# A decoder layer on one core: projection weights split six steps behind their loads, and two early output products placed behind the last value products

## The chip, the cores and the metric

The kernel runs on one core of one Trainium2 chip. The time is device microseconds of that core for one launch; of several launches the median is given. The trace is one execution taken by the hardware profiler.

## The reference, cut to what matters

One decoder layer over 2048 positions of width 1024: stick-breaking attention with 12 heads of 64, a four-head attention into 256 memory tokens, one output projection, layer norm, a squared-ReLU MLP of width 4096, and layer norm again.

```python
proj = x @ w_in_sb                      # q, k, v of 12 heads, and q_mem
z = q_block @ k.T * 64 ** -0.5          # 128 queries at a time, all earlier keys
log_stay = where(strict, log_sigmoid(-z), 0)
w = where(strict, exp(log_sigmoid(z) + sum of log_stay over the later keys), 0)
mix = w @ v
y = concat([mix, mem_out]) @ w_out
x = layer_norm(2 ** 0.25 * x + y)
x = layer_norm(2 ** 0.25 * x + square(relu(x @ w_up)) @ w_down)
```

## The kernel before, in words

Every product is done in float16 with both operands split into a high and a low half, so a weight tile that comes from memory in float32 is cut in two before TensorE (PE) may use it. `load_w` does that: it issues the load on SP's queue into a staging tile of tag "st" (three buffers), and hands two closures to `later`: `high` on ScalarE (ACT, L143), `low` one step after it on VectorE (DVE, L148). `load_cols` is its form for a 128-column piece of the input projection; `out_load`, which brings the rows of `w_out`, calls `load_w` with a 3 of its own.

Two heads are worked together as a pair p, from 0 to 5. `attention` writes the whole program of that part out by hand, step after step. One step is 128 queries of one pair against up to 512 keys: score products into two PSUM banks of tag "z" (four banks, L280), a sigmoid on ACT (L458), a scan on DVE (L466, the tile is "e"), a split of the weights on ACT and POOL (L317, L318), and a transpose by DMA from SP's queue (L319). A pair has 40 steps. Where keys and queries are of the same block, the first steps are short (128, 256, 384 keys), and some of their weights are transposed on PE (L327) and split on ACT and DVE (L161, L162, the tile is "w"). The value products (`gather`, L340, into a bank "av") of a block of keys come `BEHIND` = 4 steps after its last weights. Between the steps PE gets the projections of the next pair in portions, and the loads of the pair after that are put among them. `later(n, fn)` runs `fn` n steps on; what is due at a step is issued ahead of that step's scores. The order that results is nailed down: each instruction of an engine is tied to the one before it, on PE, DVE, ACT, POOL and SP alike.

The loads that stand inside the steps are those of the pairs 2 to 5, for v, k and q: twelve (names sv, wv and so on in the trace; sv2 is the staging tile of pair 2's value weights, wv2 its split halves).

Steps are counted through all segments, N of them. At step N, behind the last scores, `tail` issues the first 21 of 24 products of four output tiles (op12_0, op12_1, op13_0, op13_1; L670), which need all heads but the last pair, into the four "z" banks. The value products of the last block (av5_3) follow at step N + 4. Then DVE adds the end values (L301, the tile "om"), ACT and DVE split it (the tile m5_3), and the last three products of each output tile use it.

From there on the program is not written by hand: the building tool orders it by a simulated time of its own. It holds the rest of the output tiles (op14, op15, which need a "z" bank each that DVE has emptied, L677), the layer norms (L599 to L634), the left operands of the MLP (`left_operands`: sums "os" on DVE and POOL, transposes "ot" on PE at L732, evictions "op" on ACT at L161 and on DVE at L162), and the splits of the first MLP weights (L713, L714; "rt" from wu, "wr" from wd). The MLP's first product (upa, L830) uses PSUM banks that are given out anew, so it stands behind the last of these evictions.

Of the kernel before, what the change touches and what calls it, by code (L numbers as in the profile page):

```python
# [34 lines left out]
def trunk_layer(ctx: ExitStack, tc: tile.TileContext, x, mem, w_in, w_kv, w_out,  # L35
# [70 lines left out]
    def later(n, fn):  # L106
        if clock[0] is None:
            fn()
        else:
            due.setdefault(clock[0] + n, []).append(fn)  # L110

    def run(work):
        for _ in work:
            pass
# [17 lines left out]
    def load_w(key, src, shape, n, tag="ws"):  # L132

        s = sbt("st", shape, F32, f"s{key}")
        w = sbt(tag, [P, 2, D], F16, f"w{key}")
        W[key] = w
        with early():
            nc.sync.dma_start(s, src)
        flat = s if len(shape) == 2 else s.rearrange("p k f -> p (k f)")

        def high():
            with early():
                A.activation(w[:, 0, :], flat, AF.Copy, scale=SW)  # L143
                later(1, low)

        def low():
            with early():
                V.scalar_tensor_tensor(w[:, 1, :], flat, SW, w[:, 0, :], ALU.mult, ALU.subtract)  # L148

        later(n, high)  # L150

    def load_cols(w, c0, key, n=3):

        load_w(key, w[:, c0:c0 + P].rearrange("(k p) f -> p k f", p=P), [P, KT, P], n)

# [188 lines left out]
    def mem_attend():  # L344
        for hp in range(MP):
            load_cols(w_in, 3 * SBW + hp * P, f"qm{hp}")
            for c in range(NC):
                run(q_chunk(f"qm{hp}", c, f"qm{hp}_{c}"))
# [96 lines left out]
    def score(pair):  # L445

        t = pair[0]
        for u in pair:
            u.z = pst("z", "z" + u.name)
        score_pair([u.z[:, :t.W] for u in pair], qq[f"q{t.p}_{t.c}"], t.i,  # L450
                   lambda j: kk[t.p][j][:, t.pc * C:t.pc * C + t.W], not t.diag)
        if t.diag:
            for u in pair:
                T.matmul(u.z[:, t.W - P:t.W], lhsT=idb, rhs=mask, start=False, stop=True)

    def stay(pair):
        for t in pair:
            A.activation(t.z[:, :t.W], t.z[:, :t.W], AF.Sigmoid, scale=-SCORE)  # L458
# [3 lines left out]
    def scan(pair):  # L462
        for t in pair:
            t.e = sbt("et", [P, C], F32, "e" + t.name)
            init = SP if t.diag else carries[t.p, t.c, t.pc + 1][:, t.i, t.h:t.h + 1]
            V.tensor_tensor_scan(t.e[:, t.W - 1::-1], t.z[:, t.W - 1::-1], zero[:, 0:1].broadcast_to([P, t.W]), init,  # L466
                                 ALU.mult, ALU.add)
# [3 lines left out]
    def spread(pair):  # L471
        t = pair[0]
        key = t.p, t.c, t.pc
        if t.i == 0:
            carries[key] = sb.tile([P, TB, 2], F32, name="carry", bufs=3)
            for h in range(2):
                weights[key, h] = sbt("pw", [P, TB, 2 * TB, P], F16, f"w{t.p}_{t.c}_{t.pc}_{h}")
        if t.diag and t.i not in DMA_DIAG:
            turn_short([weights[key, h][:, t.i] for h in range(2)], [u.e[:, :t.W] for u in pair], "t" + t.name)
        for u in pair:  # L480
            if not t.diag or t.i in DMA_DIAG:
                turn(weights[key, u.h][:, t.i], u.e[:, :t.W], "t" + u.name)
            if t.pc > 0:
                A.activation(carries[key][:, t.i, u.h:u.h + 1], u.e[:, 0:1], AF.Copy)
# [3 lines left out]
    def gather(p, c, pc, sblk):  # L488

        if pc == c and sblk == 0:  # L490
            sums[p, c] = pst("av", f"av{p}_{c}")
        vt = vv[p, pc // 2]
        av_step(sums[p, c], lambda h, j: vt[:, pc % 2, j, sblk, h * HD:(h + 1) * HD],
                lambda h, j: weights[(p, c, pc), h][:, :, 2 * sblk + j, :],
                sblk if pc == c else 0, pc == c and sblk == 0, pc == 0 and sblk == TB - 1)
        if pc == 0 and sblk == TB - 1:
            later(1, lambda: store_mix(sums[p, c], c, p, f"m{p}_{c}", vend[p][:, c * TB:(c + 1) * TB]))
# [6 lines left out]
    BEHIND = 4  # L504

    def attention(segments, tail):

        first = nc.cur_bb.bb.instructions[-1] if nc.cur_bb.bb.instructions else None  # L510
        steps, starts = [], {}
        for blocks, done, units in segments:
            mine = [[Score(p, c, pc, h, i) for h in range(2)] for p, c in blocks for pc in range(c, -1, -1)
                    for i in range(TB)]
            starts[len(steps)] = units, len(mine), done
            steps += mine
        N = len(steps)
        share = [SHARE[0][t.i] if t.diag else SHARE[1] for t, _ in steps]
        own = [OWN[0][t.i] if t.diag else OWN[1] for t, _ in steps]
        for n, (t, _) in enumerate(steps):  # L520
            if t.i == TB - 1 and n + 1 + BEHIND < N:
                own[n + 1 + BEHIND] += VALUES[0] if t.diag else VALUES[1]

        def deal(begin, count, total):


            mine = range(begin, begin + count)
            low, high = 0, 10 * (total + sum(own))
            for _ in range(60):
                rate = (low + high) / 2  # L530
                parts = [max(0, rate * share[n] - own[n]) for n in mine]
                low, high = (rate, high) if sum(parts) < total else (low, rate)
            return [sum(parts[:k + 1]) for k in range(count)]

        work, spent, total = None, 0, 0
        for n in range(-1, N + BEHIND + 3):
            clock[0] = n
            if n in starts:
                if work is not None:
                    run(work)  # L540
                units, count, done = starts[n]
                begin, spent, total = n, 0, sum(k for k, _ in units)
                plan = deal(n, count, total / done)
                work = (cost for _, u in units for cost in u())
            for fn in due.pop(n, []):
                fn()
            if n + 1 < N:
                score(steps[n + 1])
                stay(steps[n + 1])
            if 0 <= n < N:  # L550
                scan(steps[n])
            if 0 <= n - 1 < N:
                spread(steps[n - 1])
                t = steps[n - 1][0]
                if t.i == TB - 1:
                    for sblk in range(TB):
                        later(BEHIND, lambda t=t, sblk=sblk: gather(t.p, t.c, t.pc, sblk))
            if work is not None:
                while spent < min(total, plan[min(n - begin, len(plan) - 1)]):
                    cost = next(work, None)  # L560
                    if cost is None:
                        spent = total
                        break
                    spent += cost
                if n >= N:
                    run(work)
            if n == N:
                tail()
        n += 1
        while due:  # L570
            clock[0] = n
            for fn in due.pop(n, []):
                fn()
            n += 1
        clock[0] = None
        ins = nc.cur_bb.bb.instructions
        last = {}
        on = first is None
        for i in ins:
            if on and i.engine in ENGINES:  # L580
                if i.engine in last:
                    tc.add_manual_dep(i, last[i.engine].name, ISSUE, reason="in order")
                last[i.engine] = i
            on = on or i is first
# [423 lines left out]
    def qkv_load(p, what):  # L1008
        return once(load_cols, w_in, {"q": 0, "k": SBW, "v": 2 * SBW}[what] + p * P, f"{what}{p}")
# [11 lines left out]
    for c in range(NC):  # L1021
        if c < len(kv_work):
            fn, hp, c0, nm = kv_work[c]
            load_cols(w_kv, c0, nm)
            fn(hp, nm)
        load_x(c)
# [73 lines left out]

    lastly = [out_proj((NC - 1) * TB + i, n) for i in range(TB) for n in range(NH)]

    def tail():
        free_banks[0] = ("z",)
        for work in lastly[:4]:
            for _ in range(3 * (NKO - 1)):
                next(work)

    attention(segments, tail)
    ops = {}  # L1110
    hot[0] = 1
# [12 lines left out]
    for half in range(NC // 2):  # L1124
        if half == 0:
            load_gb(g2, b2, [(gbs[:, 0], gbs[:, 1]), (gbs[:, 2], gbs[:, 3])])
        for f0 in range(0, NFP, GROUP):
# [16 lines left out]
            work = down(half, len(fps), hl, wr, f0 == 0, last)  # L1144
# [44 lines left out]
```

## Time and profile before

| | |
|---|---|
| median of 3 runs | 2434.29 us (2431.82 to 2435.8) |
| the profiled execution's own time | 2430.05 us |
| its span | 2428.3 us |
| PE busy | 2237.2 us (92%) |
| DVE busy | 1709.7 us (70%) |
| ACT busy | 1185.7 us (49%) |
| POOL busy | 1021.7 us (42%) |
| TensorE's mean granted clock | 0.975 of full speed |

The busy shares are means over stages with different limits. The steps of attention run from about 204 to 1073 us, the output projection's end and the start of the MLP from there to about 1200 us, the MLP to the end. A matmul's end is modelled, so a busy PE is not a PE at its peak; its waits are read from the times between its instructions.

### The profile page before, as it was taken

How to read it: one execution, taken by the hardware profiler on the slowest of the kernel's cores; microseconds unless marked ns; L12 is line 12 of the kernel's file. 1: busy time of each engine (PE TensorE's matmuls, PEld its weight loads, DVE VectorE, ACT ScalarE, POOL GpSimd, SP SyncE). 2: the span in 40 equal slices, each digit the busy share in tenths (PEclk: the TensorE clock that was granted, in tenths of full speed). 3: DMA queues.
4: the chain of work that ended last, by engine and by line, in shares of the span. 5: the costliest groups of instructions: out<-in, count | busy, mean ns of one | idle time of the engine just before them, and what ended most of it. 6: DMA issues, size and time to landing. Idle time of an engine off the chain costs nothing.

```text
span 2428.3 us, 34523 instructions
## 1 busy us (share of the span) xinstructions
PE 2237.2 (92%) x12032; PEld 1000.8 (41%) x12032; DVE 1709.7 (70%) x2385; ACT 1185.7 (49%) x2577; POOL 1021.7 (42%) x826
## 2 busy tenths in 40 slices
PE   7798999999989999997799999999997999999996
PEld 4343434344334343333344444444443444444443
DVE  4456777777776777779987888888676454555447
ACT  4456677776766656544544454445433322233321
POOL 0001656566564556564654456443443122211124
PEclk9899999999999999998999999999998999999998
DMA  7244888879887787876643445334565333323211
GB/s 260 44 85 90 154 162 152 162 137 163 150 160 143 165 173 170 167 178 183 220 165 114 142 152 182 133 115 149 169 194 190 105 109 96 108 87 96 96 44 70
DMA packets 606285, 342.03 MB, mean 141 GB/s; under 512 B 487840, under 2 KB 544672, under 8 KB 606112
## 3 DMA queue, kind: packets, MB, share of 16 engines
q1 hardware_dynamic: 606112, 339.84, 55.8%
q8 instruction: 94, 1.54, 0.3%
q14 instruction: 79, 0.65, 0.1%
HBM read 143.65 MB, written 77.59 MB: 91 GB/s over the span
## 4 chain that ended last, share of the span: by engine, by line
PE 58%; DVE 18%; issue 8%; ACT 7%; DMA 5%; POOL 3%; SPq 0%; ACTq 0%; DVEq 0%; POOLq 0%
PE dnb L906 7%; PE upb L830 7%; PE dnc L906 5%; PE dna L906 5%; PE upc L830 5%; PE upa L830 4%; PE pq L252 4%; PE z L280 4%; PE op L670 4%; PE av L340 3%; PE kp L252 3%; PE vp L252 3%; DVE wr L714 2%; DVE e L466 2%; POOL t L318 2%
## 5 line engine op out<-in xcount | busy, mean ns | idle before, releaser
L318 POOL TENSOR_TENSOR t<-e,t 128x512 f16<-128x512 f32 (+1 forms) x384 | 431.6, 1150 | 360.0 <-ACT t L317 293.0
L830 PEld LDWEIGHTS <-rt 128*128 128x128 f16 x2688 | 266.2, 99 | 387.7 <-issue 81.1
L906 PEld LDWEIGHTS <-hl 128*128 128x128 f16 x2736 | 267.4, 98 | 335.5 <-DVE hl L841 11.2
L466 DVE TENSOR_TENSOR_SCAN e<-z,carry,zero 128x512 f32<-128x512 f32 x288 | 350.4, 1265 | 44.5 <-ACT z L458 30.2
L921 POOL TENSOR_TENSOR acc<-acc,v 128x512 f32<-128x512 f32 x112 | 149.9, 1341 | 503.1 <-DVE acc L919 432.4
L458 ACT ACTIVATE z<-z 128x512 f32<-128x512 f32 (+1 forms) x480 | 226.6, 513 | 229.5 <-PE z L280 123.7
L830 PE MATMUL upb<-op,rt 128*128 128x512 f16 x1152 | 269.6, 383 | 13.0 <-DVE u L874 6.9
L906 PE MATMUL dnb<-wr,hl 128*128 128x512 f16 x1008 | 236.1, 380 | 0.0
L317 ACT ACTIVATE t<-e 128x512 f16<-128x512 f32 (+1 forms) x384 | 225.9, 616 | 7.7 <-DMA w<-t 6.9
L280 PE MATMUL z<-k,q 64*128 64x512 f16 (+3 forms) x1440 | 186.0, 349 | 32.3 <-DVE e L466 31.7
L830 PE MATMUL upa<-op,rt 128*128 128x512 f16 x768 | 184.8, 389 | 26.3 <-ACT u L863 19.3
L830 PE MATMUL upc<-op,rt 128*128 128x512 f16 x768 | 183.7, 387 | 16.1 <-DVE u L869 16.1
L670 PE MATMUL op<-wo,mx 128*128 128x512 f16 x720 | 171.6, 387 | 1.8 <-DVE acc L677 1.8
L466 DVE TENSOR_TENSOR_SCAN e<-z,zero 128x128 f32<-128x128 f32 (+1 forms) x192 | 147.0, 806 | 32.1 <-ACT z L458 24.9
L906 PE MATMUL dna<-wr,hl 128*128 128x512 f16 x672 | 155.0, 380 | 9.7 <-DVE hl L841 9.7
L906 PE MATMUL dnc<-wr,hl 128*128 128x512 f16 x672 | 161.1, 379 | 1.8 <-ACT hl L713 1.1
L340 PE MATMUL av<-w,v 128*64 128x512 f16 (+3 forms) x1440 | 145.9, 349 | 4.5 <-DMA w<-t 4.5
L252 PE MATMUL vp<-xT,wv 128*128 128x512 f16 x576 | 140.4, 388 | 0.0
L252 PE MATMUL pq<-xT,wq 128*128 128x512 f16 x576 | 138.7, 385 | 0.0
L252 PE MATMUL kp<-xT,wk 128*128 128x512 f16 x576 | 136.0, 380 | 0.0
L836 ACT ACTIVATE u<-u 128x512 f32<-128x512 f32 x96 | 60.3, 628 | 132.9 <-DVE u L874 78.6
L280 PEld LDWEIGHTS <-q 64*128 64x128 f16 x1440 | 55.4, 94 | 148.7 <-issue 104.7
(177 smaller groups left out, 3248.0 us busy)
## 6 DMA issues: line engine op xcount, KB each, us to landing
keptdown<-wr SPq DMA_DIRECT2D x106, 256.0 KB, 2.5
wr<-keptdown SPq DMA_DIRECT2D x106, 256.0 KB, 2.9
keptup<-rt SPq DMA_DIRECT2D x48, 512.0 KB, 3.0
rt<-keptup SPq DMA_DIRECT2D x48, 512.0 KB, 3.6
wu<-in_w_up_dram SPq DMA_DIRECT2D x32, 512.0 KB, 4.6
wd<-in_w_down_dram SPq DMA_DIRECT2D x32, 512.0 KB, 4.0
x<-in_x_dram SPq DMA_DIRECT2D x16, 512.0 KB, 10.3
acc<-in_x_dram SPq DMA_DIRECT2D x16, 512.0 KB, 5.2
```

What stands on the lines that cost most here:

```text
L252: T.matmul(pp, lhsT=wt[:, a, k, :], rhs=xs(xT, c, b, k), start=n == 0, stop=n == 3 * KT - 1)
L280: T.matmul(banks[h], lhsT=q[rows, a, i * P:(i + 1) * P], rhs=keys(b)[rows], start=n == 0, stop=stop and n == 2)
L317: A.activation(hi, src, AF.Copy)
L318: G.tensor_tensor(lo, src, hi, ALU.subtract)
L340: T.matmul(av[h * HD:(h + 1) * HD, i0 * P:].rearrange("p (t n) -> p t n", n=P), lhsT=vv(h, a), rhs=pT(h, b)[:, i0:, :], start=first and n ...
L458: A.activation(t.z[:, :t.W], t.z[:, :t.W], AF.Sigmoid, scale=-SCORE)
L466: V.tensor_tensor_scan(t.e[:, t.W - 1::-1], t.z[:, t.W - 1::-1], zero[:, 0:1].broadcast_to([P, t.W]), init, ALU.mult, ALU.add)
L670: T.matmul(pp, lhsT=lhs, rhs=W[f"o{k}"][:, kb, n * C:(n + 1) * C], start=m == 0, stop=m == 3 * NKO - 1)
L830: T.matmul(bv, lhsT=r[:, a, k, :], rhs=operand(ops, s, b, k), start=start and n == 0, stop=n == 3 * HB - 1, skip_group_check=not start)
L836: A.activation(t, t if src is None else src, AF.Relu, scale=math.sqrt(SH) / (SX * SW))
L906: mm = T.matmul(bank, lhsT=hl[s][:, g, a, i * P:(i + 1) * P], rhs=wr[r][:, g, b, :], start=start and m == 0, stop=m == 3 * n - 1, skip_gro ...
L921: G.tensor_tensor(sl, sl, u, ALU.add)
```

## The change

Two edits. The split of a piece of the input projection is due six steps behind its load and not three (only loads inside the steps are moved by it, those ahead of attention have no steps to wait for). And of the four early output products two stay at step N, and two go to step N + 4, behind the value products that are due there.

```diff
-    def load_cols(w, c0, key, n=3):
+    def load_cols(w, c0, key, n=6):
...
             if n == N:
-                tail()
+                tail(0)
+            if n == N + BEHIND:
+                tail(1)
...
-    def tail():
+    def tail(k):
         free_banks[0] = ("z",)
-        for work in lastly[:4]:
+        for work in lastly[2 * k:2 * k + 2]:
             for _ in range(3 * (NKO - 1)):
                 next(work)
```

Lines of the changed kernel are two higher from L568 on. First, ACT's order at the end of pair 0's steps, before (z is a sigmoid on scores, t the high half of weights to be transposed, named by pair, query block, key block, step and head):

```order
L317 ACTIVATE t0_3_0_0_1_3647<-e0_3_0_0_1_3612 128x4x128
L143 ACTIVATE wq2_3565<-sq2_3564 128x1024
L458 ACTIVATE z0_3_0_3_0_3663<-z0_3_0_3_0_3663 128x512
L458 ACTIVATE z0_3_0_3_1_3664<-z0_3_0_3_1_3664 128x512
L317 ACTIVATE t0_3_0_1_0_3677<-e0_3_0_1_0_3636 128x4x128
L317 ACTIVATE t0_3_0_1_1_3681<-e0_3_0_1_1_3638 128x4x128
L458 ACTIVATE z1_0_0_0_0_3693<-z1_0_0_0_0_3693 128x128
```

The same place in the changed kernel:

```order
L317 ACTIVATE t0_3_0_1_1_3678<-e0_3_0_1_1_3636 128x4x128
L143 ACTIVATE wk2_3485<-sk2_3484 128x1024
L458 ACTIVATE z1_0_0_0_0_3690<-z1_0_0_0_0_3690 128x128
L458 ACTIVATE z1_0_0_0_1_3691<-z1_0_0_0_1_3691 128x128
L317 ACTIVATE t0_3_0_2_0_3706<-e0_3_0_2_0_3670 128x4x128
L317 ACTIVATE t0_3_0_2_1_3710<-e0_3_0_2_1_3672 128x4x128
L458 ACTIVATE z1_0_0_1_0_3739<-z1_0_0_1_0_3739 128x256
L458 ACTIVATE z1_0_0_1_1_3740<-z1_0_0_1_1_3740 128x256
L317 ACTIVATE t0_3_0_3_0_3755<-e0_3_0_3_0_3702 128x4x128
L317 ACTIVATE t0_3_0_3_1_3759<-e0_3_0_3_1_3704 128x4x128
L143 ACTIVATE wq2_3563<-sq2_3562 128x1024
L259 ACTIVATE q1_2_3356<-pq1_3_3565 128x512
```

The split of wk2 stood 16 rows further up and now stands ahead of the next pair's first, short sigmoid (128 keys); wq2 stands 12 rows further on. DVE's halves move likewise. SP's order is the same in both kernels up to the last transposes of attention and the first MLP loads.

Second, DVE's order behind m5_3, before (acc12 <- op12_0 is the first eviction of an output tile, by which its "z" bank comes free):

```order
L745 TENSOR_TENSOR os0_1_0_12611<-acc5_10796 128x512
L162 SCALAR_TENSOR_TENSOR op0_3_1_12556<-ot0_3_0_12580,op0_3_0_12555 128x512
L714 SCALAR_TENSOR_TENSOR ot0_4_0_12576<-os0_0_1_12564,ot0_4_0_12576 128x512
L714 SCALAR_TENSOR_TENSOR ot0_1_0_12587<-acc0_9441,ot0_1_0_12587 128x512
L677 SCALAR_TENSOR_TENSOR acc12_12278<-acc12_12278,op12_0_12387 128x512
L677 SCALAR_TENSOR_TENSOR acc12_12278<-acc12_12278,op12_1_12409 128x512
```

The same place in the changed kernel:

```order
L716 SCALAR_TENSOR_TENSOR ot0_1_0_12587<-acc0_9441,ot0_1_0_12587 128x512
L716 SCALAR_TENSOR_TENSOR ot0_2_0_12599<-acc4_10616,ot0_2_0_12599 128x512
L636 TENSOR_TENSOR acc10_11856<-acc10_11856,gb1_0_10474 128x512
L748 TENSOR_TENSOR os0_1_1_12612<-os0_1_0_12611,acc1_9921 128x512
L636 TENSOR_TENSOR acc10_11856<-acc10_11856,gb1_1_10475 128x512
L636 TENSOR_TENSOR acc11_12033<-acc11_12033,gb1_0_10474 128x512
L636 TENSOR_TENSOR acc11_12033<-acc11_12033,gb1_1_10475 128x512
L747 TENSOR_TENSOR os0_2_0_12659<-acc6_11077 128x512
L716 SCALAR_TENSOR_TENSOR rt0_0_12977<-wu0_0_1_12960,rt0_0_12977 128x512
L716 SCALAR_TENSOR_TENSOR ot0_4_1_12624<-os0_1_1_12612,ot0_4_1_12624 128x512
L716 SCALAR_TENSOR_TENSOR ot0_1_1_12635<-acc1_9921,ot0_1_1_12635 128x512
L679 SCALAR_TENSOR_TENSOR acc12_12278<-acc12_12278,op12_0_12387 128x512
```

Counted from the sum om5_3 on DVE, that eviction was the 15th row behind it and is the 23rd now. The split of wu0_0_1, which stood right ahead of om5_3, is one of the rows that went in between; the eviction op0_0_1 (of the first transposes ot0_0_0) has gone from behind om5_3 to the row before the split of wu0_0_0. From om5_3 to the last eviction of the left operands (op0_6_1 <- ot0_6_3) there are 72 rows in both kernels. On PE the 24 value products av5_3 stand behind the 21 products of op12_1, with the four transposes ot0_0_0 between, and the 42 products of op13_0 and op13_1 behind them.

## Rows read from the trace of the kernel before

**Rows 1.** Windows: busy us (x instructions) by engine, then granted clock, DMA share, GB/s

```profile
core 0: us, PE busy (x) PEld busy (x) DVE busy (x) ACT busy (x) POOL busy (x), PEclk, DMA share, GB/s
180.00:740.00 560.00, 516.29 (x3406) 218.52 (x3404) 427.10 (x515) 390.37 (x1023) 318.28 (x286) 0.99 0.81 148
1097.00:1149.00 52.00, 35.59 (x169) 19.13 (x170) 51.90 (x76) 21.93 (x39) 23.35 (x16) 0.83 0.67 169
```

**Rows 2.** ACT's waits, 300 to 740 us: in total, times, longest; two timeline rows

```profile
ACT wk L143 <- DMA sk<-in_w_in_sb_dram: 9.1, 3, 3.8
ACT wv L143 <- DMA sv<-in_w_in_sb_dram: 7.6, 4, 2.8
ACT wq L143 <- DMA sq<-in_w_in_sb_dram: 5.0, 3, 2.6
...
320.55 1.06 ACT L143 ACTIVATE wv<-sv 128x1024 f16<-128x1024 f32 x1 [2.20 <-DMA sv<-in_w_in_sb_dram]
...
451.98 1.06 ACT L143 ACTIVATE wv<-sv 128x1024 f16<-128x1024 f32 x1 [1.46 <-DMA sv<-in_w_in_sb_dram]
```

**Rows 3.** PE's waits in 319 to 341, 452 to 470, 594 to 600, 689 to 696

```profile
PE z L280 <- DVE e L466: 2.8, 4, 0.8
...
PE z L280 <- DVE e L466: 1.6, 2, 0.8
...
PE z L280 <- DVE e L466: 0.8, 1, 0.8
...
PE z L280 <- DVE e L466: 5.0, 2, 4.3
```

**Rows 4.** Windows: the eight us behind the longest of these waits

```profile
694.00:702.00 8.00, 7.32 (x28) 2.83 (x28) 6.01 (x9) 3.29 (x11) 2.12 (x2) 0.57 0.76 135
```

**Rows 5.** L148's durations (ns), and PE's timeline behind the unwaited pair wk4, wq4

```profile
L148 DVE SCALAR_TENSOR_TENSOR wq<-sq,wq x4: 1225/1226/2179, 339.6 to 690.1; 128x1024 f16<-128x1024 f32 x4
...
670.44 0.80 PE L280 MATMUL z<-k,q 64*128 64x512 f16 x5 [0.27 <-DVE e L466]
...
673.03 0.37 PE L280 MATMUL z<-k,q 64*128 64x512 f16 x1 [1.03 <-DVE e L466]
674.20 0.80 PE L280 MATMUL z<-k,q 64*128 64x512 f16 x5 [0.80 <-DVE e L466]
```

**Rows 6.** PE's timeline, first short steps of pair 1

```profile
348.50 0.63 PE L327 MATMUL pt<-idf,e 128*128 128x128 f32 x4 [1.13 <-DVE w L162]
```

**Rows 7.** PE's timeline from the early output products to the MLP

```profile
1075.20 1.47 PE L670 MATMUL op<-wo,mx 128*128 128x512 f16 x6
...
1093.43 2.78 PE L340 MATMUL av<-w,v 128*64 128x512 f16 x24
...
1112.15 2.72 PE L670 MATMUL op<-wo,mx 128*128 128x512 f16 x6 [1.16 <-DVE acc L677]
...
1137.15 1.03 PE L670 MATMUL op<-wo,m 128*128 128x512 f16 x4
...
1148.92 1.44 PE L830 MATMUL upa<-op,rt 128*128 128x512 f16 x3 [4.11 <-DVE op L162]
```

**Rows 8.** The last two DMA transposes of attention's weights: issue, and us to landing

```profile
L319 SPq DMA_TRANSPOSE w<-t x2: 1286/1286/1287, 1088.1 to 1089.4; - x2
...
DMA to landing us min/median/max: 3.1/3.2/3.3
```

**Rows 9.** DVE's timeline from the last sum om to the last eviction

```profile
1097.04 0.69 DVE L714 SCALAR_TENSOR_TENSOR rt<-wu,rt 128x512 f16<-128x512 f32 x1 [0.75 <-ACT rt L713]
1097.65 0.68 DVE L301 SCALAR_TENSOR_TENSOR om<-av,vend 128x512 f32<-128x512 f32 x1
...
1111.42 1.87 DVE L677 SCALAR_TENSOR_TENSOR acc<-acc,op 128x512 f32<-128x512 f32 x3
...
1148.23 0.64 DVE L162 SCALAR_TENSOR_TENSOR op<-ot,op 128x512 f16<-128x512 f32 x1
```

**Rows 10.** The first w_down rows: issue on SP, split on ACT

```profile
1137.35 0.33 SPq L889 DMA_DIRECT2D wd<-in_w_down_dram  x1
...
1140.84 0.63 ACT L713 ACTIVATE wr<-wd 128x512 f16<-128x512 f32 x1
```

## The prediction

> **What bounds the kernel now.** I began with busy time by stretches, because the two edits lie in stages with different limits. From 180 to 740 us PE is busy 516 of 560 us and DVE 427 [rows 1]: here PE sets the pace, and what may be won is the time in which it waits. From 1097 to 1149 us it is the other way: DVE is busy 51.90 of 52 us, PE 35.59 [rows 1]. That stretch is as long as DVE's list of work, and work moved on PE counts only where it makes DVE wait.
>
> Next I read ACT's waits, since the first edit concerns instructions that wait for a load. Ten of the twelve splits inside the steps found their load not landed: 9.1, 7.6 and 5.0 us, together 21.7 us, the longest 3.8 [rows 2]. ACT takes its instructions in order, so the next sigmoid stands behind that wait, behind it DVE's scan, and behind that the next scores, which need a bank the scan has read. So the question is how much of the 21.7 us reaches PE. Its waits for the scan just behind these splits are 2.8, 1.6, 0.8 and 5.0 us [rows 3], 10.2 us; the rest is swallowed by the four banks. The last has a sequel: behind a wait of 4.3 us the granted clock in 694 to 702 us is 0.57, so most of that stretch ran at 1.2 and not 2.4 GHz [rows 4]. PE was busy 7.32 us there, and 7.32 x (1 - 0.57) = 3.1 us of it is the price of the low clock.
>
> **Six steps instead of three.** The same split of two neighbouring pairs is 451.98 - 320.55 = 131.4 us apart [rows 2], 40 steps, so a step is 3.3 us and three more are 9.9 us. The longest wait was 3.8, so every load has landed by then. Removed: 10.2 + 3.1 = 13.3 us of PE's time.
>
> The work itself stays, 1.06 us on ACT [rows 2] and 1.23 on DVE [rows 5] for each split, and it lands somewhere else. Its price with no wait in it can be bounded. Above: wk4 and wq4 are the two splits that waited for nothing, and behind them PE waited 0.27 + 1.03 + 0.80 = 2.1 us for DVE [rows 5], 1.05 each. Below: nothing, as ACT and DVE have a quarter of the stretch free [rows 1]. Between these I go by the place. wv2 and wv3 take the places that wk2 and wk3 had, long steps: 0. Three pairs (wk2 with wq2, wk3 with wq3, wv4 with wv5) now fall into the first short steps of the next pair of heads, where PE already waits 1.13 us for the split of w on DVE [rows 6]. The ACT work stands ahead of that split, while DVE has gaps between the short scans; I take two thirds of 2.1, 1.4 us for each pair, 4.2 together. wk5 with wq5 is charged the full 2.1; wk4 with wq4 only changes its place. Together 6.3, and at most 10 x 1.05 = 10.5 us. So the first edit gives 13.3 - 6.3 = 7.0 us, between 2.8 and 13.3. The staging buffers stand this: three loads share three tiles, and only wq5 could find its tile (wk4's) still unsplit, with a margin of a few us.
>
> **Two products behind the value products.** The 84 early products fill 1075.20 to 1093.43 us [rows 7], and the value products start at once. Half of them end 9.1 us earlier, at 1084.3. But the value products need the last transposes, issued at 1088.1 and 1089.4, landing 3.2 us later, at 1092.6 [rows 8]. That comes from SP's queue, which the edit leaves as it is. So PE would stand still for about 8 us, and start again on the low clock as it did at 694 us [rows 4]: the 24 products, 2.78 us at full speed [rows 7], would take some 5.5, started by the transpose before the last at 1091.3, and end near 1097. The sum om that needs them starts at 1097.65 today [rows 9]. Up to here: 0. On the high clock, om would start about 1.4 us earlier, as the split ahead of it with its wait (0.75 and 0.69) has left [rows 9].
>
> Behind om DVE is full, with 72 rows to the last eviction in both orders, so the end at 1148.23 + 0.64 [rows 9] only moves if DVE waits for something new. There is one place. The first eviction of an output tile is eight rows later, at 0.6 to 0.7 us for most rows about 6 us: 1117.4 and not 1111.42 [rows 9]. PE's next output product, which needs that bank, started at 1112.15 and the four were done at 1138.2 [rows 7], 26 us; now from 1118 to 1144. Behind them DVE has seven rows, and one is the split of the first w_down rows, whose staging tile is the one op15 has just read. Its load was issued at 1137.35 and split on ACT at 1140.84 [rows 10], 3.5 us later. 1144 + 3.5 + 0.6 on ACT, and five of DVE's rows at 0.6, make 1151 against 1148.9. I take + 2.0 us, since the first MLP sums stand a little earlier in the new order. Bounds: - 1.4 (om early, no wait) and + 6 (the six us carried through). The two moved products cost PE nothing else: 35.59 us of work in 52 [rows 1] leave room for 9.1 more.
>
> **Sum.** - 7.0 + 2.0 = - 5.0 us. The profiled execution took 2430.05 us, 4.2 less than the median of the runs, 2434.29; it gives 2425.0, and for the median of runs 2429.3.
>
> **The rivals.** *The splits are paid in full.* The waits go, but each moved split costs PE its 1.05 us, because the scan has something else to wait for, first of all POOL's use of the e tiles. Then 13.3 - 10.5 = 2.8, with the tail - 0.8 us: 2433.5. For it speaks that POOL is busy 318 of 560 us [rows 1], so that a moved instruction of DVE will often lie beside one of POOL's. One of the wq splits took 2.18 us instead of 1.23 [rows 5]; the median of 1.226 speaks against it.
>
> The Trainium skill (SBUF — State Buffer, section "SBUF: two separate sides") says that VectorE with two SBUF inputs and GpSimd share a port pair, and whichever comes second is blocked for the other's whole instruction. By that rule up to ten moved halves could each be held by about an estimated 0.95 us (2.18 - 1.23), which is the 10.5 us of this rival nearly to the microsecond. The trace agrees that it happens, once in four wq splits, not that it is the rule there.
>
> *All of it comes home.* The splits fall into gaps, and om comes early: - 13.3 - 1.4, say - 13 us: 2421. For it: ACT's and DVE's free quarter. Against it: wk4 and wq4, which had no wait and still cost PE 2.1 us.
>
> *The tail eats it, the kernel is slower.* Place: the value products behind an 8 us standstill. If om comes late, then the evictions, then op14, the 9.1 us of the moved products are laid bare, with 2.8 us of the value products at the low clock and some 2 us of op13 behind them: + 14, net + 7: 2441. It decides when the tail costs over 7.0 + 4.9 = 11.9 us. Against it: DVE has 52 us of other work in that stretch, most of which needs none of these products.
>
> **How the numbers follow.** A measurement of this kernel can tell about 0.2%, 4.9 us. My forecast has a chance of 0.52 with a range of its own from 2425 to 2433 (splits 5 to 9 us, tail 0 to 4); it reaches past the bound of 4.9 us with 0.32 of these. Splits paid in full 0.20, within the bound. All of it home 0.18, faster. The tail 0.10, slower. So faster 0.50, same 0.40, slower 0.10. The range leaves out the far end of the last two: 2421 to 2436.
>
> **What would show it.** Right: the profile after has no waits of ACT's L143 for a load inside the steps, PE's waits for the scan behind them are gone, the clock at 690 to 702 us stays at 1.00, and the short steps of pairs 1, 2 and 3 show a PE wait for w above 1.13. The last steps end some 7 us earlier. Then PE waits near 8 us for the transposes ahead of av5_3, the clock is down behind it, and upa starts about 75.7 us behind the first early output product (today 1148.92 - 1075.20 = 73.7). Wrong: if PE waits for z as often as before, the stalls were not the loads'; if the value products start with no wait, the transposes came earlier than I read; if DVE shows idle time of over 3 us before upa, the tail costs more than I say.

## The result, and the profile after

The changed kernel takes 2442.9 us (median of 20 runs, 2427.87 to 2448.9), the kernel before 2429.62 (20 runs, 2417.8 to 2436.89). The ratio is 1.0055 with a 95% interval of 1.0038 to 1.0072: slower by some 13 us, where 5 us faster was forecast, outside the range of 2421 to 2436.

The two profiled executions do not show that at once: 2430.05 us before and 2432.32 after, 2.3 us apart. A stall of 12 us in the MLP, which is no part of the change, stood in the one and not in the other; it has its own section at the end. The times of each kernel lie in two clusters with it, 10 short and 10 long ones before, 7 and 13 after, so that a part of the 13 us is that share: from short to short the medians lie some 12 us apart, from long to long some 9. So I compare by stage.

**The steps of attention.** Their length is taken from the first transpose on PE to the end of the last scores: 205.88 to 1069.64 us before, 207.30 to 1081.79 after, so 863.8 and 874.5 us, 10.7 longer. The loads are no longer waited for: ACT's longest waits between 300 and 750 us, the L143 of [rows 2] gone from among them:

```profile
ACT z L458 <- PE z L280: 47.2, 30, 3.2
ACT z L458 <- PE z L454: 35.1, 18, 4.5
...
ACT t L317 <- DMA w<-t: 9.9, 13, 1.9
```

PE's waits over the whole of the steps, before (us in total, times, longest; z are scores that wait for the scan, pt transposes on PE that wait for the split of w, av value products that wait for weights transposed by DMA):

```profile
PE z L280 <- DVE e L466: 30.9, 34, 4.3
PE pt L327 <- DVE w L162: 24.0, 18, 4.5
PE av L340 <- DMA w<-t: 4.5, 6, 1.3
```

and after:

```profile
PE pt L327 <- DVE w L162: 31.1, 18, 4.5
PE z L280 <- DVE e L466: 21.6, 25, 2.2
PE av L340 <- DMA w<-t: 11.8, 11, 3.2
```

The waits for the scan fell by 9.3 us. But those for the short steps' weights w rose by 7.1, and those for transposed weights (the value products, L340) by 7.3. Over the same stretches PE's busy time, for the same 5169 matmuls, went from 803.06 to 808.08 us (columns as in [rows 1], before first):

```profile
205.88:1069.60 863.72, 803.06 (x5169) 338.78 (x5168) 660.99 (x778) 560.22 (x1423) 496.33 (x437) 0.99 0.81 154
```

```profile
207.30:1081.80 874.50, 808.08 (x5169) 340.69 (x5168) 666.20 (x778) 561.07 (x1423) 496.69 (x437) 0.98 0.81 153
```

That growth is the lower clock. In stretches of 4 us over the steps, PE's busy time times (1 - granted clock) adds up to 10.5 us before and 15.5 after, and what is left of the busy time is 792.6 and 792.5. Where the clock is low, PE's timeline after shows, at the end of pair 0:

```profile
341.03 0.59 PE L340 MATMUL av<-w,v 128*64 128x512 f16 x1 [3.20 <-DMA w<-t]
342.02 3.96 PE L340 MATMUL av<-w,v 128*64 128x512 f16 x23 [0.41 <-DMA w<-t]
...
352.80 0.63 PE L327 MATMUL pt<-idf,e 128*128 128x128 f32 x4 [3.08 <-DVE w L162]
```

PE waits for 3.20 us, then the 23 value products take 3.96 us (24 took 2.78 in [rows 7]), then PE waits 3.08 us where it waited 1.13 [rows 6]. The same happens at the end of pair 1, where the first wait is 3.00 us. The granted clock in these two places, before:

```profile
341.00:349.00 8.00, 6.87 (x59) 3.24 (x56) 6.01 (x10) 6.36 (x17) 6.73 (x6) 1.00 1.16 175
476.00:484.00 8.00, 6.87 (x53) 3.15 (x49) 5.90 (x12) 5.55 (x16) 4.43 (x4) 1.00 1.05 190
```

and after, with 690 to 702 us, where [rows 4] had shown 0.57:

```profile
341.00:349.00 8.00, 7.56 (x51) 3.10 (x52) 2.14 (x5) 3.65 (x7) 3.40 (x4) 0.79 1.10 177
476.00:484.00 8.00, 7.49 (x49) 3.54 (x50) 2.01 (x5) 3.25 (x7) 3.16 (x3) 0.79 1.12 187
690.00:702.00 12.00, 9.97 (x76) 4.31 (x74) 8.82 (x10) 8.17 (x22) 9.88 (x9) 1.00 0.98 184
```

One place on the low clock was gone and at least two came up. But the first varies without the edit: at 690 to 702 us the granted clock was 0.72 in the kernel before, 0.86 in e_tail (below), whose steps are the same, and 0.86 in e_splits, whose steps are those of the change.

**The end of attention.** PE's waits from the last scores to the MLP, after:

```profile
1104.66 0.61 PE L340 MATMUL av<-w,v 128*64 128x512 f16 x1 [7.64 <-DMA w<-t]
1105.82 4.33 PE L340 MATMUL av<-w,v 128*64 128x512 f16 x23 [0.55 <-DMA w<-t]
1132.42 2.72 PE L672 MATMUL op<-wo,mx 128*128 128x512 f16 x6 [9.20 <-DVE acc L679]
1164.51 4.00 PE L832 MATMUL upa<-op,rt 128*128 128x512 f16 x9 [4.04 <-DVE op L162]
```

and DVE's rows that answer to [rows 9]:

```profile
1110.26 0.69 DVE L301 SCALAR_TENSOR_TENSOR om<-av,vend 128x512 f32<-128x512 f32 x1 [0.65 <-PE av L340]
...
1131.70 0.67 DVE L679 SCALAR_TENSOR_TENSOR acc<-acc,op 128x512 f32<-128x512 f32 x1
```

The first early output product starts at 1087.35, so om stands 22.9 us behind it (22.45 before, [rows 7, 9]), the first eviction 21.4 behind om (13.8 before), and upa 77.2 behind the first product (73.7 before; 3.5 us more).

### The profile page after: what moved, and what is told of

The parts are those of the page before. It is cut to its first block, busy times and chain, and to the rows that moved or that the text cites. A ratio compares the mean times of both kernels' runs of the same rounds, so it can differ in the third digit from the quotient of the medians.

```text
span 2430.6 us, 34524 instructions
## 1 busy us (share of the span) xinstructions
PE 2241.2 (92%) x12032; PEld 1004.1 (41%) x12032; DVE 1709.0 (70%) x2385; ACT 1186.2 (49%) x2577; POOL 1025.4 (42%) x826
## 4 chain that ended last, share of the span: by engine, by line
PE 60%; DVE 17%; issue 7%; ACT 6%; DMA 5%; POOL 3%; SPq 0%; ACTq 0%; DVEq 0%; POOLq 0%
PE dnb L908 7%; PE upb L832 7%; PE dnc L908 5%; PE dna L908 5%; PE upc L832 4%; PE op L672 4%; PE upa L832 4%; PE pq L252 4%; PE av L340 4%; PE z L280 4%; PE kp L252 4%; DVE wr L716 3%; PE vp L252 3%; DVE e L466 2%; PE pqm L252 2%
## 5 line engine op out<-in xcount | busy, mean ns | idle before, releaser
L317 ACT ACTIVATE t<-e 128x512 f16<-128x512 f32 (+1 forms) x384 | 226.6, 617 | 13.4 <-DMA w<-t 10.5
L340 PE MATMUL av<-w,v 128*64 128x512 f16 (+3 forms) x1440 | 151.6, 357 | 20.1 <-DMA w<-t 19.9
L340 PEld LDWEIGHTS <-v 128*64 128x64 f16 x1440 | 78.8, 111 | 94.4 <-issue 41.9
L630 POOL TENSOR_TENSOR acc<-acc,gb 128x512 f32<-128x512 f32 x60 | 84.2, 1431 | 78.7 <-ACT acc L624 78.7
## 6 DMA issues: line engine op xcount, KB each, us to landing
x<-in_x_dram SPq DMA_DIRECT2D x16, 512.0 KB, 10.6
```

The source lines that it names most:

```text
L317: A.activation(hi, src, AF.Copy)
L340: T.matmul(av[h * HD:(h + 1) * HD, i0 * P:].rearrange("p (t n) -> p t n", n=P), lhsT=vv(h, a), rhs=pT(h, b)[:, i0:, :], start=first and n ...
L630: G.tensor_tensor(sl, sl, gb["g", n], ALU.mult)
```

## Experiments

The length of the steps is read in every profile as above, one profile for each kernel. It scatters: the steps of the kernel before, of e_tail and of e_late1 (both below) are the same instructions, and took 863.8, 864.0 and 867.7 us. So one length is good to some 2 to 4 us. In the same three profiles the waits for the scan were 27.8 to 30.9 us, those for transposed weights 4.5 to 6.9. Ratios are against runs of the kernel before on the same chip.

### One edit at a time

**e_splits**, the first edit without the second:

```diff
-    def load_cols(w, c0, key, n=3):
+    def load_cols(w, c0, key, n=6):
```

> First edit alone: every piece of the input projection inside the steps is split six steps behind its load, all four early output products stay at step N. Theory A (the first edit is the loss, the moved splits fall into the first short steps of a pair and what PE wins it then waits for transposed weights): 8 to 11 us slower than the kernel before, first early output product at about 1085 to 1088 us. Rival B (the loss is the second edit's, the first is worth nothing or a gain): 0 to 7 us faster, that product at 1068 to 1075 us.

**e_tail**, the second edit without the first:

```diff
-                tail()
+                tail(0)
+            if n == N + BEHIND:
+                tail(1)
...
```

> Second edit alone: splits three steps behind their loads as before, two early output products at step N and two at N + 4. Theory A: 2 to 4 us slower, upa about 77 us behind the first early output product (73.7 before). Rival B: 10 to 13 us slower, upa 83 us or more behind it.

| | median us | ratio, 95% | steps us | last scores to upa us |
|---|---|---|---|---|
| before | 2431.08 | | 863.8 | 79.3 |
| e_splits | 2437.71 | 1.0046 (1.0024 to 1.0068) | 874.1 | 80.1 |
| e_tail | 2431.26 | 0.9994 (0.9973 to 1.0015) | 864.0 | 83.2 |

The loss is the first edit's, about 11 us by the ratio. The second costs 3.9 us up to upa (83.2 against 79.3), and the MLP gives most of it back: from upa to a wait of PE for the bank of upc, for "DVE u" (at 1261.61 us before and 1263.69 here), it is 112.7 us before and 110.0 here.

```profile
1263.69 2.75 PE L832 MATMUL upc<-op,rt 128*128 128x512 f16 x12 [2.52 <-DVE u L871]
```

### How far the splits are moved, and which

**e_four** moves all splits by one step, **e_pair5** only the last two by three:

```diff
-    def load_cols(w, c0, key, n=3):
+    def load_cols(w, c0, key, n=4):
```

> Splits four steps behind their loads instead of three, no second edit. No split then stands behind a short sigmoid of the next pair; wq2, wq3 and wv5 end one step ahead of it. By theory A, if the place in the short steps is what costs, the time is that of the kernel before or 2 to 5 us better, with the waits for loads nearly gone (the longest was 3.8 us, a step is 3.3). If instead any step by which a split moves away from its load costs the same (transposes pace PE), 2 to 4 us slower.

```diff
-    def load_cols(w, c0, key, n=3):
+    def load_cols(w, c0, key):
+        n = 6 if key in ("k5", "q5") else 3
```

> Only wk5 and wq5, the last two loads, are split six steps behind their loads; everything else as before. It takes away the wait of 4.3 us at 689 us and the low clock behind it, and pays 3.2 us of waits for the scan as read in the changed kernel (0.29 + 0.97 + 1.17 + 0.81). Theory A: 3 to 6 us faster, as these two fall into long steps. Rival C (whatever PE wins in the steps it loses again to the transposes that SP's queue brings at its own pace): no difference, within 1.5 us, with new waits of PE for transposed weights behind 700 us.

e_four: 2435.99 us, ratio 1.0025 (1.0006 to 1.0045), steps 868.8. ACT's waits for loads are down from 21.7 to 2.4 us, and it is slower; 2 to 4 us had been the other theory's figure. The short steps of pairs 1 to 3 wait for w no longer than before, but I had overlooked wk5 and wq5. They stood ahead of a sigmoid of 256 keys and now stand behind it, between the scan and the first split of w, on DVE for 1.94 and 1.21 us, and PE waits 3.84 us for w there (at 698 us), where it had waited 4.26 us for the scan. Over the steps the waits for the scan are 5.2 us down, those for w 1.7 and those for transposed weights 0.9 up; PE's busy time is 6.5 us up (809.6), so most of this loss is the low clock, and which stops it lies behind is not sorted out.

e_pair5: 2432.01, ratio 1.0012 (0.9991 to 1.0032), steps 861.8: no difference that can be told, and my 3 to 6 us were wrong. The wait of 4.26 us at 689 us is gone and the waits for the scan are 5.0 us down, but a wait of 1.67 us for w has come up right there. The new waits for transposed weights that rival C had named did not come (4.9 us against 4.5).

### Loads with an eighth of the bytes

This pair separates the two things that the first edit changes: the wait for a load, and the place of the split. The loads inside the steps bring 64 KB, the split reads it eight times over; seven eighths of those weights are left out.

```diff
+        s = sbt("st", [P, 1, P], F32, f"s{key}")
...
+        nc.sync.dma_start(s, src[:, 0:1, :])
+        flat = s.broadcast_to([P, KT, P])
```

> Kernel before (three steps), but each of the twelve loads inside the steps brings only the first eighth of its piece, 64 KB instead of 512, and the split repeats it eight times at the same cost; so the numbers of pairs 2 to 5 are not the layer's. Length of the steps (first short transpose of pair 0 to the end of the last scores): 863.7 us before, 874.1 with the splits at six. Theory D (the DMA engines are full where the loads run, so the waits of ACT and later those of PE are two faces of one bound): with seven eighths of the loads' bytes gone the waits go and nothing takes their place, 850 to 855 us. Rival E (what costs is ACT's wait itself, and the loss at six comes only from the new place of the splits): also shorter, but the wait of PE for transposed weights at the ends of pairs stays at 0.7 to 1.5 us each, 851 to 857. This run gives the base for the next.

> The same small loads, with splits at six steps. Against the run before it is the price of the new places alone, with no load to wait for in either: the prediction's figure was 6.3 us (1.4 for each of three pairs of splits in the short steps, 2.1 for the last). Theory D: 5 to 8 us (2.0 for each of three pairs, as read in the changed kernel), so 6 of the loss are the place's and the remaining 3 to 5 us of the 10.4 are transposes that full DMA engines bring late. Rival E: 10 us or more, all of the loss.

| length of the steps, us | split at three | split at six | place |
|---|---|---|---|
| 512 KB loads | 863.8 | 874.1 | + 10.3 |
| 64 KB loads | 853.8 | 863.5 | + 9.7 |
| bytes | + 10.0 | + 10.6 | |

(Medians of the 64 KB kernels: 2421.31 and 2431.55 us. At three, 3.6 of ACT's 21.7 us of waits for loads are left, at six none.) The bytes cost 10 us whether the splits wait for them or not, and the place costs 10 us with large loads and with small. These are four single profiles; the ratios of the runs say the same, with 11.7 us for the bytes at three and 12.9 at six, 11.2 for the place with large loads and 10.0 with small. Theory D had said 5 to 8 for the place, rival E 10 or more; with a scatter of 2 to 4 us the 9.7 stands nearer to E in size. But E's other half, that ACT's wait is what the bytes cost, does not hold: at six steps there is none, and they still cost 10.6.

PE's waits over the steps show how. 64 KB at three:

```profile
PE pt L344 <- DVE w L179: 24.0, 18, 4.5
PE z L297 <- DVE e L483: 20.6, 28, 2.4
PE av L357 <- DMA w<-t: 4.1, 7, 1.0
```

64 KB at six:

```profile
PE pt L344 <- DVE w L179: 31.2, 19, 4.5
PE z L297 <- DVE e L483: 23.1, 27, 2.1
PE av L357 <- DMA w<-t: 5.7, 8, 1.2
```

512 KB at six (e_splits):

```profile
PE pt L327 <- DVE w L162: 31.5, 19, 4.5
PE z L280 <- DVE e L466: 23.0, 24, 2.3
PE av L340 <- DMA w<-t: 10.6, 9, 4.1
```

The wait for w depends on the place alone: 24.0 and 24.0 at three, 31.2 and 31.5 at six. The bytes at three are 10.3 us of waits for the scan (30.9 before against 20.6). At six these are not there (23.0 and 23.1); instead the wait for transposed weights is 4.9 us longer (10.6 against 5.7), and PE's busy time is 807.86 us against 802.59, so 5.3 us go to the low clock. Together 10.2 us. In e_splits the clock is down behind such waits at the ends of pairs 0 and 1 (0.79 at 338 to 346 us and at 472 to 480), as in the change.

The 9.7 us of the place with small loads are waits alone: 7.2 us more for w, 2.5 for the scan, 1.6 for transposed weights and 1.1 less elsewhere, with PE's busy time as it was (802.6 and 802.8).

Why do transposes come late? From 312 to 342 us, the end of pair 0, the view of the DMA queues before, and how long the transposes issued there took to land:

```profile
q1 hardware_dynamic: 20958, 6.14, 104.0%
...
w<-t SPq DMA_TRANSPOSE x17, 3.5
...
DMA to landing us min/median/max: 3.2/3.5/5.9
```

and with 64 KB loads, split at three:

```profile
q1 hardware_dynamic: 20028, 5.19, 97.5%
...
w<-t SPq DMA_TRANSPOSE x20, 3.3
...
DMA to landing us min/median/max: 3.1/3.3/4.9
```

The same for the splits at six, with 512 KB (e_splits) and with 64 KB:

```profile
DMA to landing us min/median/max: 3.2/3.4/6.0
...
DMA to landing us min/median/max: 3.2/3.3/4.7
```

The queue is busy nearly throughout in all four (97.5 to 105.3%). Three of the loads are issued in these 30 us, and with 512 KB the slowest transpose takes 5.9 or 6.0 us to land, with 64 KB 4.9 or 4.7, wherever the splits stand; the median is 3.3 to 3.5. At the end of pair 1 (445 to 475 us) it is 6.0 and 5.8 against 4.5 and 4.4. So the large loads hold up single transposes near them by about a microsecond or more, and it is such a transpose that the value products at a pair's end may wait for. The count of transposes issued (17 against 20 at three, 18 against 19 at six) says less, as the window cuts the two kernels at different places.

### Splits past the short steps, and loads earlier

```diff
-    def load_cols(w, c0, key, n=3):
+    def load_cols(w, c0, key):
+        n = 10 if key in ("k2", "q2", "k3", "q3", "v5") else 3
```

> Full loads; the splits of k2, q2, k3, q3 and v5 ten steps behind their loads, past the short steps of the next pair, all others at three. The waits of ACT for these five loads go (about 11 us of 21.7) and no split stands in the short steps. Theory D: nearly nothing comes of the waits since PE then waits for transposed weights at the end of the pair instead: length of the steps 862 to 866 us against 863.7. Rival E: 857 to 860 us, as the waits for the scan behind these splits go (about 4 us).

```diff
-    def load_cols(w, c0, key, n=3):
+    def load_cols(w, c0, key, n=6):
...
-            units.insert(len(units) - len(loads) + k, load)
+            units.insert(len(units) - len(loads) + k - 1, load)
```

> The loads for pairs 2 to 5 that stand at the end of a segment are issued one unit of projection work (some three steps) earlier and split six steps behind, so their splits stand where they stood before the change, or one step later; the last four loads (k4, q4, k5, q5) are as in the change. ACT's waits for loads go without any split in the short steps. Theory D: the bytes are the same and the DMA engines as full, so it gives 0 to 3 us (what the wait at 689 us gives, mostly): 860 to 864 us. Rival E: 10 us shorter, 852 to 856.

e_ten: 2436.76 us, ratio 1.0012 (0.9991 to 1.0034), steps 873.1. The ratio does not tell it from the kernel before, and the 9.3 us more in the steps of this one profile are above what its upper end allows (8 us). Both theories were wrong on the steps, and so was my aim: wk2 is clear of the first short steps, but wq2 now stands behind the sigmoid of 256 keys in the second round of short steps (at 359.84 us) and, on DVE with 1.93 us, right ahead of a split of w; PE's wait for w in the short steps is 3.7 us a pair against 2.5. This and e_four say that it is not the short sigmoid that a split must stay clear of but the splits of w. But that is the smaller part of the 9.3 us: the waits for w are 2.8 us up over the steps, those for transposed weights 5.2 (9.7 us), and PE's busy time 3.2.

e_early: 2425.03 us, ratio 0.9968 (0.9945 to 0.9991), steps 858.0: faster, between the two theories' figures for the steps (856 and 860). PE's waits over the steps:

```profile
PE pt L327 <- DVE w L162: 26.2, 19, 4.5
PE z L280 <- DVE e L466: 21.4, 26, 2.1
PE av L340 <- DMA w<-t: 5.8, 8, 1.3
PE av L340 <- issue: 1.6, 1, 1.6
```

The waits for the scan are down as in the change, that for w is only 2.2 us up, and the short steps of pairs 1 to 3 wait for w as before (1.13 us at the first). The wait for transposes grew by 2.9 us, not by 6 to 7, if the last row, whose releaser the profile does not show, is counted in. That this is because the loads now run ahead of the stretch where the pair's end needs its transposes is argued; no run separates it.

### Which half of a split is in the way

**e_dve**, on top of the first edit:

```diff
-                later(1, low)
+                later(6 if key in ("k2", "q2", "k3", "q3", "v5") else 1, low)
```

> First edit alone (splits at six), but DVE's half of the splits of k2, q2, k3, q3 and v5 comes six steps behind ACT's half instead of one, so it has left the place between the scan of 256 keys and the first split of w; ACT's half stays. Length of the steps: 863.8 us before, 874.1 with the first edit. If DVE's half is what makes the short steps late: PE's waits for w there fall from 4.5 to about 2.5 us for each pair, and the length is 867 to 870. If ACT's half is: the waits stay at 4 us or more, 872 to 875.

2436.18 us, ratio 1.0039 (1.0011 to 1.0068), steps 872.2. The wait for w in the short steps is 3.5 us a pair (4.5 with the first edit, 2.5 before), between the two figures named: half of this price goes with DVE's half, half stays. The length stays in the range for ACT's half, as PE's busy time, at 810.4 us, is 2.5 up on e_splits and takes a part of the gain back. DVE's timeline shows the same. Before, at the first short steps of pair 1:

```profile
344.74 1.27 DVE L466 TENSOR_TENSOR_SCAN e<-z,zero 128x256 f32<-128x256 f32 x2 [0.92 <-ACT z L458]
...
347.43 0.29 DVE L162 SCALAR_TENSOR_TENSOR w<-pt,w 128x128 f16<-128x128 f32 x1 [0.26 <-ACT w L161]
```

and in e_splits:

```profile
345.04 1.27 DVE L466 TENSOR_TENSOR_SCAN e<-z,zero 128x256 f32<-128x256 f32 x2 [4.88 <-ACT z L458]
347.24 1.94 DVE L148 SCALAR_TENSOR_TENSOR wq<-sq,wq 128x1024 f16<-128x1024 f32 x1 [0.93 <-ACT wq L143]
...
349.71 0.27 DVE L162 SCALAR_TENSOR_TENSOR w<-pt,w 128x128 f16<-128x128 f32 x1
```

with this on POOL beside it:

```profile
345.83 2.28 POOL L318 TENSOR_TENSOR t<-e,t 128x512 f16<-128x512 f32 x2 [3.93 <-ACT t L317]
```

From the end of the scans to w it was 347.43 - 346.01 = 1.4 us and is 349.71 - 346.31 = 3.4: 2.0 us more, PE's wait from 1.13 to 3.08. DVE waits 0.93 us for ACT's half and then needs 1.94 for its own, where the median was 1.226 [rows 5]. The Trainium skill (SBUF — State Buffer, section "SBUF: two separate sides") says that VectorE with two SBUF inputs and GpSimd lock a shared port pair against each other. The 1.94 us fit that, since POOL's two instructions last until 348.11 us, 0.87 into the split; that the port is the cause is not shown by itself. In e_splits the medians of DVE's halves inside the steps are 1.77, 1.74 and 1.94 us for wv, wk and wq, where all three were 1.226 before. So what the prediction had as a rival is the rule in the new places.

### Both, and the stall in the MLP

**e_late1** is the kernel before with one number of the last layer norm changed, **e_early_tail** the changed kernel with the earlier loads, **e_early_late1** e_early with that number:

```diff
-                ln_apply(a, mv[:, j, 0:1], rs[:, j:j + 1], 2 if tb < NT // 2 else 1)
+                ln_apply(a, mv[:, j, 0:1], rs[:, j:j + 1], 1)
```

> Kernel before with one number of the last layer norm changed: its shifts are shared between POOL and DVE for all row blocks, and not given to POOL alone for the first half. Times of both kernels lie in two clusters some 12 us apart, and in the profiles of the long ones DVE's subtraction hl lasts 13 to 15 us beside a run of POOL's gains and shifts. If POOL's run without a gap is what holds DVE, its shorter run makes the long executions rarer or the stall shorter: median 2418 to 2425 us, and no DVE instruction of over 6 us in the MLP. If the stall has another cause: two clusters as before, near 2420 and 2433.

> The changed kernel with both edits, but the loads for pairs 2 to 5 that stand at the end of a segment issued one unit of projection work earlier. Alone that placement gave steps of 858.0 us and a median about 6 us under the kernel before. The second edit alone cost 3.9 us up to upa, of which the MLP gave back nearly all. So 2421 to 2428 us at the median, steps of 857 to 859 us, upa 83 us behind the last scores.

> Loads one unit earlier with splits at six (as in the kernel whose steps took 858.0 us) together with the shifts of the last layer norm shared between POOL and DVE, whose times lay in one cluster, 2421.6 to 2429.3 us, median 2425.6. Without the stall of 12 us that comes and goes, what the earlier loads are worth is to be read off the medians: if the 4 to 6 us seen in the steps of two profiles are real, 2419 to 2422 us, in one cluster; if they were chance, 2424 to 2427.

e_late1: 2425.61 us, 2421.6 to 2429.26 in ten runs, one cluster; ratio 0.9997 (0.9976 to 1.0019). e_early_tail: 2426.26, ratio 0.9987 (0.9957 to 1.0018), steps 860.6, 83.0 us from the last scores to upa: as expected in the median, a little longer in the steps (857 to 859 expected), and not to be told from the kernel before. e_early_late1: 2418.29 us, ratio 0.9958 (0.9941 to 0.9976), steps 862.5 in its one profile: the fastest version found, ahead of both kernels. A good part of that ratio is the stall that is gone: 12 of the 17 runs of the kernel before beside it were long ones (2431 to 2439 us), and against the five short ones, 2420.4 to 2422.7, its median is 3.5 us shorter. The three profiles with the earlier loads have steps of 858.0, 860.6 and 862.5 us, mean 860.4, the three with the steps of before 865.2: some 5 us.

## Why the prediction was wrong

**The waits of ACT and their weight for PE: right as far as read.** They went, and PE's waits for the scan fell by 7.9 us in e_splits, where 10.2 less the 2.1 charged for wk5 and wq5, 8.1, had been forecast. With a scatter of 3 us in these waits, so close a match is in part luck.

**The step that failed: "Removed: 10.2 + 3.1 = 13.3 us of PE's time".** Four terms of the ledger, forecast against e_splits (sums of its waits and busy time less those of before):

| us | forecast | measured |
|---|---|---|
| waits for the scan | - 8.1 | 23.0 - 30.9 = - 7.9 |
| waits for w | + 4.2 | 31.5 - 24.0 = + 7.5 |
| waits for transposed weights | 0 | 10.6 - 4.5 = + 6.1 |
| busy, by the clock | - 3.1 | 807.86 - 803.06 = + 4.8 |
| sum | - 7.0 | + 10.5 (steps: + 10.3) |

The third and fourth rows are what the step left out: 14.0 of the 17.5 us between the sums. I asked how much of ACT's wait reaches PE, and took what reached it as won. I did not ask what else would be late at the same time. The loads that ACT waited for also hold up transposes on the same queue, and PE's value products wait for those a few us on. The wait for the scan and the wait for transposes were two readings of one bound, of which the first, being earlier, hid the second. The loads with an eighth of the bytes show it: 10 us either way. The low clock at 694 us was priced as the cost of that one wait and taken as won for good. Both came from one execution: in e_tail, with the same steps, the waits that made up 5.0 us there are 1.66 and 0.77, and the clock at 694 to 702 us is 0.79 and not 0.57. And after the change PE stood for 3.2 us at the end of pair 0 and 3.0 at that of pair 1, and the clock was down behind both. Of the 6.1 us up to 2.4, and of the 4.8 us up to 3, may be scatter (4.5 to 6.9 us of waits for transposed weights and 803.1 to 806.2 us of busy time among the three profiles with the steps of before).

**"4.2 together" for the short steps: mis-sized.** 1.4 us a pair was forecast, 2.0 measured (4.5 against 2.5 of waits for w in each of three pairs). A further 1.6 us of waits for w came up at 703 us, ahead of the new place of wk5 and wq5; it stands in e_pair5 and e_early too, where these splits no longer wait for a load, so the wait for the scan had hidden another. The whole of the place is 9.7 us with small loads, where 6.3 were taken and 10.5 were the upper bound. On this term the rival "the splits are paid in full" was right; its 13.3 of gain was not.

**The second edit: right in its mechanism, a little low in size.** PE stood still for 7.64 us (about 8 forecast), the 23 value products took 4.33 us on the low clock (some 5.5 forecast for 24), om stood where it had, and the first eviction came 21.4 - 13.8 = 7.6 us later (6 forecast). upa stood 77.2 us behind the first early product (75.7 forecast), 3.5 us more than before where 2.0 were forecast, DVE idle for less than 3 us behind om. Alone it made no difference that could be measured.

**The rivals.** The one on the slower side had the sign but not the place: it put the loss in the tail, which cost next to nothing. A slower outcome by the first edit was not among them, since the upper bound of its price, 10.5, lay below 13.3; the bound on the gain was missing. Of the place, the wait for w is the largest part (7.2 of 9.7 us with small loads). Left open is whether the rest, 2.5 us for the scan and 1.6 for transposed weights less 1.1 elsewhere, follows from it or is scatter, and which stop each part of the low clock lies behind.

## What to carry to other kernels

A wait that is taken away is worth what stands next in line, so look in the same stretch for other waits on the same resource: here single transposes beside the loads took 5.9 us to land and not 3.5, in the trace before already. The loads' bytes cost 10 us wherever the work that waits for them stood; moving the loads themselves earlier gave some 5 us. Before work is moved into a latency chain (here the short steps' splits of w), read what stands directly ahead of the chain's links on each engine: here it cost 2.0 us for each pair of splits.

## What the runs showed of the hardware

**One DVE instruction held for 12 us by a run of POOL's.** Times of both kernels lie in two clusters some 12 us apart (the kernel before: 2416 to 2424 and 2429 to 2438 in most runs). In nine of the twelve profiles with the layer norm as it was, one subtraction on DVE in the MLP lasted 12.9 to 15.5 us, and from upa to the end of the span it was 1277 to 1282 us; in the other three, the changed kernel's among them, no DVE instruction there took over 6 us, and it was 1265 to 1266. Before:

```profile
1827.23 13.82 DVE L841 TENSOR_TENSOR hl<-r,hl 128x512 f16<-128x512 f32 x1 [8.69 <-ACT r L839]
...
1830.70 9.81 POOL L634 TENSOR_TENSOR acc<-acc,gb 128x512 f32<-128x512 f32 x8
```

After:

```profile
1840.38 1.65 DVE L843 TENSOR_TENSOR hl<-r,hl 128x512 f16<-128x512 f32 x1 [8.66 <-ACT r L841]
```

DVE's instruction ended 0.5 us behind the last of POOL's row of instructions, and in between POOL had run eleven of them without a gap; after, DVE's got in between two. Before, PE then waited 9.2 us for hl. With half of that row's shifts given to DVE (e_late1, e_early_late1) no such instruction was in the profiles, and the times of e_late1 were one cluster of 8 us. That supports POOL's run as what holds DVE; what the two share there no run shows. It costs as well: without the stall it is 1271 to 1272 us from upa to the end with that number changed, against 1265 to 1266, and e_late1's median is that of the kernel before (ratio 0.9997).

**The clock over the same work.** The busy time of the same matmuls of the steps was 801.8 to 810.4 us in the fourteen profiles, without any change in them. Busy time times (1 - granted clock), in stretches of 4 us, was 10.4 to 20.8 us, and what is left 789.6 to 792.6 in all of them, so nearly all of the difference is the clock. Not every stop brought it down: behind PE's wait of 3.08 us for w after the change it stood at 1.00 (349 to 357 us), behind the 3.20 us shortly before at 0.79 (341 to 349).
